# Pinning the order of sixteen seven-product units, with their input sums moved to VectorE and their SBUF pools laid out anew

## The chip, the core and the metric

The kernel runs on one core of one Trainium2 chip. The metric is the device time of one execution in microseconds. The core has TensorE (matrix products, written to eight banks of PSUM), VectorE (DVE in the profile), ScalarE (ACT), GpSimd (POOL) and queues that start transfers between memory and SBUF (SP's and GpSimd's here). Each engine takes its instructions in one fixed order, and waits at an instruction until what it needs is there.

## The reference, cut to what matters

Two layers over 1024 latent tokens and 256 context tokens, with 1024 features. The first layer is attention beside an mLSTM; the change lies at the start of the second, odd layer:

```python
def _c_mixer(h_lat, h_ctx, w_in, lb, h_norm, w_out, need_ctx):
    def project(h):
        q, f_fwd, f_bwd, i, z = _split_cols(h @ w_in, C_SIZES)   # five blocks of 2048 columns

        def decay(f_pre):
            f = lb + (1.0 - lb) * jax.nn.sigmoid(f_pre.astype(F32))
            return _bht(_heads(1.0 - f, HG_HEADS)), _bht(_heads(jnp.log(f), HG_HEADS))

        rec = (_bht(_heads(jax.nn.silu(q), HG_HEADS)), _bht(_heads(i, HG_HEADS)), (decay(f_fwd), decay(f_bwd)))
        return rec, z
    ...
```

`h` is the normed and modulated input of the layer. The part concerned computes two of the five blocks, `q` (with its SiLU, for the latent tokens) and `f_fwd` (with sigmoid and lower bound, for all tokens), for all 16 heads of 128 columns. The other blocks are computed later, head by head.

## The kernel before, in words

**Products in three parts.** Every float32 product is made of three matmuls on a split of each operand into a high and a low part: `split` (L68 on) writes the high part with a cast on ScalarE (L73) and the low part with a subtraction on VectorE (L74). `dense` issues, for each block of 128 features, high x high (L131), low x high and high x low (L132, L133). The input `h` lies split and transposed in SBUF as `hh` and `hl`, [128, 8, 1280]: eight blocks of 128 features, 1024 latent tokens and 256 context tokens.

**The stage in front.** The first layer ends with ten output tiles of 128 tokens, in the order 8, 9 (context), 4, 5, 6, 7, 0, 1, 2, 3. `out_tile` computes one: the products, then on VectorE `og` (L959, reads the bank) and the new `ox` (L960). `norm` makes `nx` (a square with sum on ScalarE, two small GpSimd instructions for the root, a scaling on VectorE, L282), and `mod_tr` transposes it on TensorE (L294) and writes `ntmp`, from which `h_sink` writes `hh` (ScalarE, L317) and `hl` (VectorE, L318). Tokens 0 to 511 come last; token tile 3 is the last of all. The weights of these products lie in the pool `wo1` (28 tiles), the other tiles of the stage in `op0`.

**The seven-product phase** (`hg_wide`). For `q` and `f_fwd` the latent tokens are cut in two halves of 512 (t = 0, 1), the 1024 features in two halves (c = 0, 1), and two heads' columns make a pair: a product of 2 x 2 blocks, done with seven block products in place of eight (Strassen's scheme in Winograd's form). One unit is one pair of heads of one kind; 16 units run in the order f, q, f, q, ... In each:

- P1 = X(0,0) by weight block (0,0) into bank `a`; the copy `p1` (L1151, ScalarE) keeps it; P2 = X(0,1) by block (1,0) is added into `a`, which then is output block (0,0).
- P4 = X(1,1) by the weight form t4 into a bank `d`.
- P6 = S2 by t2 into a bank `b`; VectorE makes `u2` = b + p1 (`add`, L1054); P7 = S3 by t3 is added into `b`; `u3` = b + p1. Output block (1,0) is d + u3.
- P5 = S1 by t1 into a bank `c`; output block (1,1) is c + u3; P3 = S4 by block (1,1) is added into `c`; output block (0,1) is c + u2.
- An f unit also computes its context tokens from the raw weight blocks, in four parts of 12 matmuls of 256 columns (`cpart`, bank `tr`), behind P1, P2, before P3 (C1 in the diff) and behind P3. A q unit has none.

A block product is 12 matmuls of 512 columns. Each result goes through a sigmoid on ScalarE, one instruction on VectorE and a transfer by GpSimd's queue to memory (`finish`), with tiles `co` from a ring of two.

S1 to S4 are sums of quarters of `h`, [128, 4, 512] each, split in `st1` to `st4` (h and l). `half_sums` computes them at the start: S1 = A(1,0) + A(1,1), S2 = S1 - A(0,0), S3 = A(0,0) - A(1,0), S4 = A(0,1) - S2, each A being hh + hl. S1, S2 and S4 run on VectorE (28 instructions, L1022 and L1024) in `gF`'s free half and two tiles; S3 runs on GpSimd (12 instructions). The weight forms t1 to t4 are differences of raw weight blocks, computed on GpSimd (`raws`, L1078) in a ring `br` of 11 tiles, and split into a ring of four slab pairs in the pool `w1`, three ahead of the product that uses them (`more`).

**Order.** Instructions are traced in program order; a scheduler with a model of the engines then decides the order of each engine's queue. It takes what its model says is ready, earlier traced work first; `urgent()` puts a block ahead of all other. `seg()` fixes an order: what it encloses on TensorE is issued after `last_pe`. Before, `last_pe` is None during `hg_wide`, so the order of the products is the scheduler's choice. `hg_f` traces three gate parts of head 0 (context, tokens 512 to 1023, tokens 0 to 511) ahead of the phase.

**Pools.** `st` (S1 to S4, 64 KB a partition) and `sx` (`br`, `u2`, `u3`, `co`, `p1`) are laid over the bytes of `op0` and `wo1`, in the order in which their tiles are first asked for; with `reuse_waits="tile"` a new tile waits only for the old tiles under it. The next pool, `hg`, lies over `st` and `sx` in turn. The banks of PSUM are two `mm`, two `tr` and four of the current phase (`x` here, then `s`); a phase's pool has no such option before.

Of the kernel before, what the change touches and what calls it, by code (L numbers as in the profile page):

```python
# [10 lines left out]
F32 = mybir.dt.float32  # L11
# [3 lines left out]
ALU = mybir.AluOpType  # L15
# [30 lines left out]
class Prog:  # L46
# [929 lines left out]
    def hg_f(self, h, pool, w=None):  # L976
# [8 lines left out]
        def part(t0, n):  # L985
# [3 lines left out]
            if self.pinned:  # L989
                self.last_pe = m  # L990
# [20 lines left out]
    def half_sums(self, pool, tp, F):  # L1011
        nc = self.nc
        hh, hl = self.hh, self.hl
        S = {n: [self.t(pool, [P, 4, 512], F32R, f"st{n}{c}", 1) for c in "hl"] for n in (4, 3, 1, 2)}
        x = [F[:, 0, 0:512], F[:, 0, 512:1024]] + [self.t(tp, [P, 512], F32, n, 1) for n in ("u2", "u3")]
# [31 lines left out]
        return S  # L1047


    def hg_wide(self, sp, tp, F):  # L1050
# [15 lines left out]
        def raws(kind, i):  # L1066
# [9 lines left out]
            def sub(x, y, out=None):  # L1076
                o = self.t(tp, [P, 512], F32, "br", self.brs) if out is None else out
                nc.gpsimd.tensor_tensor(out=o, in0=x, in1=y, op=ALU.subtract)  # L1078
# [9 lines left out]
        order = lambda kind: [(0, 0), (1, 0), "t4", "t2", "t3", "t1"] + ([(0, 1)] if kind == "f" else []) + [(1, 1)]  # L1088
        queue = [(u, n) for u in range(len(units)) for n in order(units[u][0])]
        rawd, forms = {}, {}  # L1090

        def more(n):
            for u, f in queue[:n]:
                if u not in rawd:
                    rawd[u] = raws(*units[u])
                hi, lo = [self.t(self.wp, [P, 512], F32R, "w" + c, self.slabs) for c in "hl"]
                self.split(hi, lo, rawd[u][f])
                forms[(u, f)] = _W([hi], [lo], 4, P)
            del queue[:n]

        more(3)
        S = self.half_sums(sp, tp, F)
        for u, (kind, i) in enumerate(units):
            def form(n):
                more(1)
                return forms.pop((u, n))

            def finish(t, c, x):
                h = 2 * i + c
                o = self.t(tp, [P, 512], F32, "co", 2)  # L1110
# [17 lines left out]
            def cpart(c, w, k0, stop):  # L1128
                if kind == "q":
                    return  # L1130
                if c not in ctx:
                    ctx[c] = self.ps("tr", [P, CTX])
                self.dense(
                    ctx[c], w.h, w.l, lambda k: hh[:, k0 + k, LAT:T], lambda k: hl[:, k0 + k, LAT:T], 4, not stop, stop
                )
                if stop:
                    h = 2 * i + c
                    o = self.t(tp, [P, 512], F32, "co", 2)[:, 0:CTX]
# [7 lines left out]
            p1, u2, u3 = [self.t(tp, [P, 512], F32, n, 2 if n == "p1" else 1) for n in ("p1", "u2", "u3")]  # L1146
            pa, pd = [self.ps("mm", [P, 512]) for _ in range(2)]
            pb, pc = [self.ps("x", [P, 512]) for _ in range(2)]
            w = form((0, 0))
            prod(pa, w, (0, 0), True)  # L1150
            nc.scalar.copy(p1, pa)  # L1151
            cpart(0, w, 0, False)
            w = form((1, 0))
            prod(pa, w, (0, 1), False)
            finish(0, 0, pa)
            cpart(0, w, 4, True)
            prod(pd, form("t4"), (1, 1), True)
            prod(pb, form("t2"), 2, True)
            add(u2, pb, p1)
            prod(pb, form("t3"), 3, False)  # L1160
            add(u3, pb, p1)
            tail(1, 0, pd, u3, p1)
            prod(pc, form("t1"), 1, True)
            tail(1, 1, pc, u3, u3)
            if kind == "f":
# [953 lines left out]
```

## Time and profile before

| | |
|---|---|
| Median of 3 runs | 3346.03 us (3344.75 to 3347.75) |
| Profiled execution, its own time | 3344.65 us |
| Span of that execution | 3342.7 us, 64833 instructions, mean clock 0.996 |
| Busy: TensorE (PE), its weight loads (PEld) | 3288.8 us (98%), 2921.1 us (87%) |
| Busy: VectorE, ScalarE, GpSimd | 2178.8 us (65%), 1457.4 us (44%), 833.3 us (25%) |
| Last output product ends, phase begins | about 1787 us |
| Phase ends, first strips of the next stage | about 2183 us, 2188 us |

In the lists of the profile, a group names the line of the code, the engine, the operation, the tile written and the tiles read ("out<-in"), then a count; times are microseconds from the start of the span, means of one instruction nanoseconds. A bracket at the end of a row of the timeline gives the idle time in front of the instruction and what ended it. The granted clock of TensorE is a share of its full clock. Matmuls overlap: one of 512 columns is listed with 0.39 us while the next starts 0.23 us after it. L1054 is `add`, L1151 the copy `p1`, L1071 the loads of raw weights.

### The profile page before, as it was taken

To read this page: it belongs to the slowest core of one execution; us is meant where nothing else is said; L and a number is where in the kernel's file an instruction comes from. 1 tells how busy PE (TensorE), PEld (TensorE's weight loads), DVE (VectorE), ACT (ScalarE), POOL (GpSimd) and SP (SyncE) were. 2 spreads that over 40 slices of the span, in tenths; PEclk is the share of its full clock that TensorE was granted. 3 is DMA by queue.
4 is the path that set the end of the run, shared out by engine and by line. 5 is a ranking of instruction groups with operands and counts; after the bars stand their busy time and mean duration, and the time that the engine had idled before them with its cause. 6 is when DMAs were issued, how large, how long until landed. Compare 5 with 4: busy or idle time off the path is not lost.

```text
span 3342.7 us, 64833 instructions
## 1 busy us (share of the span) xinstructions
PE 3288.8 (98%) x24814; PEld 2921.1 (87%) x24814; DVE 2178.8 (65%) x4965; ACT 1457.4 (44%) x3389; POOL 833.3 (25%) x1215
## 2 busy tenths in 40 slices
PE   7999999999999999999998999999999999999999
PEld 6699899988989888898886888889999999999977
DVE  5337666666655566787668654577677677677756
ACT  5335554455444444455454333333333433433443
POOL 2222222212211112221104433202322323233110
PEclk9999999999999999999999999999999999999999
DMA  7713222232233444444652333222322324334376
GB/s 247 243 51 85 85 70 81 68 94 82 75 89 102 149 125 123 132 134 144 214 170 77 106 104 104 92 80 77 110 85 93 113 81 111 94 85 107 92 210 163
DMA packets 338101, 379.80 MB, mean 114 GB/s; under 512 B 34600, under 2 KB 269800, under 8 KB 336768
## 3 DMA queue, kind: packets, MB, share of 16 engines
q1 hardware_dynamic: 286032, 236.73, 24.0%
q0 software_dynamic: 51760, 138.94, 13.3%
q8 instruction: 195, 3.19, 0.4%
q14 instruction: 114, 0.93, 0.1%
HBM read 272.31 MB, written 103.08 MB: 112 GB/s over the span
## 4 chain that ended last, share of the span: by engine, by line
PE 90%; DMA 3%; issue 2%; DVE 2%; ACT 1%; POOL 1%; SPq 1%; ACTq 0%; POOLq 0%; DVEq 0%
PE mm L131 16%; PE mm L132 16%; PE mm L133 16%; PE s L1295 4%; PE mm L923 3%; PE mm L924 3%; PE mm L925 3%; PE acc L861 2%; PE tr L841 2%; PE acc L633 2%; PE s L642 2%; PE x L133 2%; PE x L131 2%; PE x L132 2%; PE s L1366 1%
## 5 line engine op out<-in xcount | busy, mean ns | idle before, releaser
L131 PE MATMUL mm<-wh,hh 128*128 128x256 f32 (+1 forms) x1504 | 465.0, 309 | 2.1 <-DVE graw L1588 0.8
L132 PE MATMUL mm<-wl,hh 128*128 128x256 f32 (+1 forms) x1504 | 462.8, 308 | 0.0
L133 PE MATMUL mm<-wh,hl 128*128 128x256 f32 (+1 forms) x1504 | 460.2, 306 | 0.0
L131 PE MATMUL mm<-hh,wh 128*128 128x512 f32 (+1 forms) x1160 | 424.3, 366 | 4.7 <-DVE og L959 3.1
L133 PE MATMUL mm<-hh,wl 128*128 128x512 f32 (+1 forms) x1160 | 419.6, 362 | 0.6 <-DVE wl L74 0.6
L132 PE MATMUL mm<-hl,wh 128*128 128x512 f32 (+1 forms) x1160 | 419.4, 362 | 0.6 <-DVE hl L318 0.6
L131 PEld LDWEIGHTS mm<-wh,hh 128*128 128x128 f32 x1504 | 283.9, 189 | 21.5 <-ACT ev L352 3.4
L132 PEld LDWEIGHTS mm<-wl,hh 128*128 128x128 f32 x1504 | 283.9, 189 | 12.4 <-issue 0.7
L133 PEld LDWEIGHTS mm<-wh,hl 128*128 128x128 f32 x1504 | 283.7, 189 | 12.0 <-issue 0.5
L131 PE MATMUL mm<-wzh,hh 128*128 128x256 f32 x960 | 280.8, 293 | 0.0
L132 PE MATMUL mm<-wzl,hh 128*128 128x256 f32 x960 | 271.3, 283 | 0.0
L133 PE MATMUL mm<-wzh,hl 128*128 128x256 f32 x960 | 271.2, 282 | 0.0
L131 PEld LDWEIGHTS mm<-hh,wh 128*128 128x128 f32 x1160 | 218.7, 189 | 41.0 <-ACT ev L371 4.2
L133 PEld LDWEIGHTS mm<-hh,wl 128*128 128x128 f32 x1160 | 218.4, 188 | 34.4 <-DVE wl L74 1.3
L132 PEld LDWEIGHTS mm<-hl,wh 128*128 128x128 f32 x1160 | 218.9, 189 | 31.5 <-DVE hl L318 1.4
L131 PEld LDWEIGHTS mm<-wzh,hh 128*128 128x128 f32 x960 | 183.5, 191 | 2.0
L132 PEld LDWEIGHTS mm<-wzl,hh 128*128 128x128 f32 x960 | 184.1, 192 | 0.0
L133 PEld LDWEIGHTS mm<-wzh,hl 128*128 128x128 f32 x960 | 183.6, 191 | 0.0
L74 DVE TENSOR_TENSOR wl<-wraw,wh 128x512 fp32r<-128x512 f32 x176 | 120.2, 690 | 82.7 <-ACT wh L73 80.5
L1325 DVE TENSOR_TENSOR gQ<-gQ,gF 128x1024 f32<-128x1024 f32 x112 | 149.0, 1331 | 29.9 <-PE s L1295 29.9
L1330 ACT COPY gksel<-gK 128x1024 f32<-128x1024 f32 x96 | 110.3, 1149 | 119.4 <-DVE gK L1325 55.0
L73 ACT CAST wh<-wraw 128x512 fp32r<-128x512 f32 x176 | 107.7, 620 | 96.6 <-PE mm L132 24.6
(559 smaller groups left out, 8468.0 us busy)
## 6 DMA issues: line engine op xcount, KB each, us to landing
wraw<-in_wab_dram SPq DMA_DIRECT2D x108, 256.0 KB
wraw<-yd SPq DMA_DIRECT2D x92, 256.0 KB
br<-in_wc_dram SPq DMA_DIRECT2D x64, 256.0 KB
md<-ev POOLq DMA_DIRECT2D x60, 256.0 KB, 2.6
wraw<-in_wc_dram SPq DMA_DIRECT2D x120, 128.0 KB
mloz<-md SPq DMA_DIRECT2D x40, 256.0 KB
s<-gyt POOLq DMA_DIRECT2D x36, 256.0 KB, 5.2
adar<-in_wada_dram SPq DMA_DIRECT2D x16, 512.0 KB
```

Of the source, the lines that this page charges most:

```text
L73: m = nc.scalar.copy(hi, x)
L74: nc.vector.tensor_tensor(out=lo, in0=x, in1=hi.bitcast(F32), op=ALU.subtract)
L131: mm(ps, lhsT=lh(k), rhs=rh(k), start=(start and k == 0), stop=False, skip_group_check=skip)
L132: mm(ps, lhsT=lh(k), rhs=rl(k), start=False, stop=False, skip_group_check=skip)
L133: m = mm(ps, lhsT=ll(k), rhs=rh(k), start=False, stop=(stop and k == nk - 1), skip_group_check=skip)
L633: nc.tensor.matmul(num, lhsT=qc[:, j, :], rhs=C[d][:, j, :], start=False, stop=(j == 1))
L923: mm(ps, lhsT=yh[k], rhs=w.h(kk), start=(kk == 0), stop=False)
L924: mm(ps, lhsT=yh[k], rhs=w.l(kk), start=False, stop=False)
L925: mm(ps, lhsT=yl[k], rhs=w.h(kk), start=False, stop=(kk == 8 * len(qs) - 1))
L1295: return self.nc.tensor.matmul(out[s], lhsT=lhsT, rhs=rhs, start=True, stop=True, tile_position=(0, b * 64))
L1325: nc.vector.tensor_tensor(out=v, in0=v, in1=tot, op=ALU.mult)
L1330: m = nc.scalar.copy(ksel.rearrange("p (b s i) -> p b s i", s=2, i=h), pick(K))
```

## The change

It does six things.

1. S3's 12 instructions run on VectorE (`chain(nc.vector, ...)`), and so do the four differences of unit 0's raw weights; those of the other units stay on GpSimd.
2. `half_sums` becomes a generator in three stages: places for the sums, then S1's sums, then everything else, traced at three points.
3. The four forms for P4, P1, P2 of unit 0 and P1 of unit 1 are split first, as urgent work, into the bytes that `st4` takes afterwards. The other forms go through the ring of slabs as before, in the order of the new list `steps`; two are traced ahead, and one more at each product.
4. Every product, every context part and the gate parts of head 0 stand in `seg()`: TensorE's order is that of `steps`. Unit 0 begins with P4, both parts of C0 (its first context column), the gate part F for tokens 0 to 511, P1, P2; then come P1 and P2 of unit 1; then P6, P5, P7, C1, P3 of unit 0, the rest of unit 1, and from unit 2 on P1, P2, P4, P6, P7, P5, (C1), P3 unit by unit. In unit 0 the addition for output block (1,1) is made after P7.
5. `st2`, `st3`, a pad of 256 bytes, `co`, `p1` and `u2` lie in `st`; `st1`, `st4`, `br` and `u3` in `sx`. `co`, `p1`, `u2` and `u3` are asked for where they are first used.
6. The phase pools of PSUM get `reuse_waits="tile"`.

The diff, cut:

```diff
@@ hg_f, part()
-            if self.pinned:
-                self.last_pe = m
+            self.last_pe = m
@@ half_sums
-        S = {n: [self.t(pool, [P, 4, 512], F32R, f"st{n}{c}", 1) for c in "hl"] for n in (4, 3, 1, 2)}
-        x = [F[:, 0, 0:512], F[:, 0, 512:1024]] + [self.t(tp, [P, 512], F32, n, 1) for n in ("u2", "u3")]
+        two = lambda n: [self.t(pool if n in (2, 3) else tp, [P, 4, 512], F32R, f"st{n}{c}", 1) for c in "hl"]
+        S = {n: two(n) for n in (2, 3, 1)}
+        self.t(pool, [P, 64], F32, "pad", 1)
+        yield two(4)
+        S[4] = two(4)
+        x = [F[:, 0, 0:512], F[:, 0, 512:1024]] + [
+            self.t(tp, [P, 512], F32, "u3", 1), self.t(tp, [P, 512], F32, "br", self.brs)
+        ]
...
             chain(nc.vector, x[j], h, (l, add), (h2, add), (l2, add))
+        yield
+        for j in range(4):
             done(1, j, x[j])
...
-            y = self.t(tp, [P, 512], F32, "co", 2)
-            chain(nc.gpsimd, y, h, (l, add), (h2, sub), (l2, sub))
+            y = self.t(pool, [P, 512], F32, "co", 2)
+            chain(nc.vector, y, h, (l, add), (h2, sub), (l2, sub))
...
-        return S
+        yield S
@@ hg_wide
         def prod(ps, w, n, first):
             x = X(n)
-            self.dense(ps, w.h, w.l, x[0], x[1], 4, first, True, True)
+            with self.seg():
+                self.last_pe = self.dense(ps, w.h, w.l, x[0], x[1], 4, first, True, True)
...
-                nc.gpsimd.tensor_tensor(out=o, in0=x, in1=y, op=ALU.subtract)
+                eng.tensor_tensor(out=o, in0=x, in1=y, op=ALU.subtract)
...
+        order = lambda kind: ["P1", "P2", "P4", "P6", "P7", "P5"] + (["C1"] if kind == "f" else []) + ["P3"]
+        form_of = dict(P1=(0, 0), P2=(1, 0), P4="t4", P6="t2", P7="t3", P5="t1", C1=(0, 1), P3=(1, 1))
+        steps = [(0, n) for n in ("P4", "C0", "F", "P1", "P2")] + [(1, "P1"), (1, "P2")]
+        steps += [(0, n) for n in ("P6", "P5", "P7", "C1", "P3")] + [(1, n) for n in order("q")[2:]]
+        steps += [(u, n) for u in range(2, len(units)) for n in order(units[u][0])]
...
+        def split_form(u, n, hi, lo):
+            if u not in rawd:
+                rawd[u] = raws(*units[u], *([nc.vector] if u == 0 else []))
+            self.split(hi, lo, rawd[u][form_of[n]])
+            forms[(u, n)] = _W([hi], [lo], 4, P)
+
+        sums = self.half_sums(sp, tp, F)
+        spare = next(sums)
+        for i, (u, n) in enumerate(((0, "P4"), (0, "P1"), (0, "P2"), (1, "P1"))):
+            with self.urgent():
+                split_form(u, n, *[t[:, i, :] for t in spare])
+        queue = [x for x in steps if x[1] in form_of and x not in forms]
...
-        more(3)
-        S = self.half_sums(sp, tp, F)
-        for u, (kind, i) in enumerate(units):
+        more(2)
+        next(sums)
...
+            def P1():
+                t["a"] = self.ps("mm", [P, 512])
+                t["p1"] = self.t(sp, [P, 512], F32, "p1", 2)
+                w = form("P1")
+                prod(t["a"], w, (0, 0), True)
+                nc.scalar.copy(t["p1"], t["a"])
+                if u:
+                    cpart(0, w, 0, False)
+
+            def P2():
+                w = form("P2")
+                prod(t["a"], w, (0, 1), False)
+                finish(0, 0, t["a"])
+                if u:
+                    cpart(0, w, 4, True)
...
+            def P6():
+                t["b"] = self.ps("x", [P, 512])
+                t["u2"] = self.t(sp, [P, 512], F32, "u2", 1)
+                prod(t["b"], form("P6"), 2, True)
+                add(t["u2"], t["b"], t["p1"])
+
+            def P7():
+                t["u3"] = self.t(tp, [P, 512], F32, "u3", 1)
+                prod(t["b"], form("P7"), 3, False)
+                add(t["u3"], t["b"], t["p1"])
+                tail(1, 0, t["d"], t["u3"], t["p1"])
+                if u == 0:
+                    c22()
...
+        todo = {}
+        for u, n in steps:
+            if u not in todo:
+                todo[u] = unit(u, *units[u])
+            todo[u][n]()
+            if (u, n) == (0, "F"):
+                S = next(sums)
@@ build
-                self.last_pe, self.pinned = None, False
+                self.last_pe = None
                 FF = self.hg_f(0, None, wf)
-                for part in FF[2]:
+                for part in FF[2][:2]:
                     part()
...
-                    self.hg_wide(sp, tp, FF[0])
+                    self.hg_wide(sp, tp, FF[0], FF[2][2])
@@ _Banks.phase
-        with self.tc.tile_pool(name="ps" + "".join(tags), bufs=1, space=PSUM) as pool:
+        with self.tc.tile_pool(name="ps" + "".join(tags), bufs=1, space=PSUM, reuse_waits="tile") as pool:
```

P3, P4, P5 and C1 are written as functions in the same way, with the instructions that they had. `cpart`'s matmuls stand in `seg()` too, and its `co` tile comes from `sp`.

More of the change, by code (lines that the diff above doesn't have):

```diff
@@ new lines, in c22, with P5, C1, P3 @@
+            def c22():
+                tail(1, 1, t["c"], t["u3"], t["u3"])
+            def P5():
+                t["c"] = self.ps("x", [P, 512])
+                prod(t["c"], form("P5"), 1, True)
+                if u:
+                    c22()
+            def C1():
+                cpart(1, form("C1"), 0, False)
+            def P3():
+                w = form("P3")
+                prod(t["c"], w, 4, False)
+                tail(0, 1, t["c"], t["u2"], t["u2"])
+                cpart(1, w, 4, True)
```

60 lines of the change are left out of this document (19 added, 41 removed).

## The prediction

> **What bounds the kernel now.** I read the page first, then the busy time by windows around the seven-product phase, then what TensorE waited for there, then the engines' timelines.
>
> ```profile
> PE 90%; DMA 3%; issue 2%; DVE 2%; ACT 1%; POOL 1%; SPq 1%; ACTq 0%; POOLq 0%; DVEq 0%
> ```
>
> The chain that ended last is TensorE for 90%, so a microsecond of TensorE idleness inside the phase is a microsecond of the time. The windows show where the phase has any (window, length, then busy time of PE, PEld, DVE, ACT, POOL, then the granted clock):
>
> ```profile
> 1787.00:1863.00 76.00, 60.19 (x271) 47.99 (x270) 68.72 (x93) 32.02 (x66) 41.71 (x30) 0.91 0.20 62
> 1960.00:2160.00 200.00, 200.00 (x979) 168.37 (x978) 102.59 (x158) 69.79 (x121) 68.55 (x78) 1.00 0.31 101
> 2176.00:2194.00 18.00, 12.90 (x112) 10.80 (x111) 14.76 (x25) 6.18 (x10) 2.05 (x3) 0.82 0.55 176
> 1802.00:1805.00 3.00, 2.92 (x10) 2.40 (x11) 1.18 (x3) 1.61 (x5) 0.63 (x1) 0.50 0.00 0
> 1830.00:1840.00 10.00, 7.48 (x19) 5.80 (x20) 10.00 (x13) 3.06 (x7) 3.91 (x3) 0.53 0.20 59
> ```
>
> Three stages. The seam into the phase (1787 to 1863) has 15.8 us without a matmul and two stretches at half clock. The body (1960 to 2160) has none at all: 200.00 of 200.00 at clock 1.00. The seam out (2176 to 2194) has 5.1 us. So a better seam can win, and the body can only lose. The waits of TensorE in the first seam:
>
> ```profile
> PE x L132 <- DVE st2l L74: 6.5, 2, 5.3
> PE mm L131 <- DVE og L959: 3.1, 1, 3.1
> PE tr L294 <- DVE nx L282: 3.1, 1, 3.1
> PE x L133 <- DVE wl L74: 1.3, 1, 1.3
> PE mm L131 <- ACT p L1151: 1.0, 1, 1.0
> PE mm L132 <- DVE hl L318: 0.6, 2, 0.3
> PE mm L133 <- DVE wl L74: 0.3, 1, 0.3
> ```
>
> All but one end on VectorE. The half clock costs 2.92 x 0.50 + 7.48 x 0.47 = 5.0 us more. Seam in: 15.9 + 5.0 = 20.9 us that a perfect change could take away.
>
> **The change, part by part.** *Sums and raw differences to VectorE.* The first row is TensorE's first matmul after the last output product; the others show what VectorE does while GpSimd (POOL) works, and after it has stopped:
>
> ```profile
> 1787.10 0.28 PE L131 MATMUL mm<-hh,wh 128*128 128x256 f32 x1
> 1785.51 5.97 POOL L1078 TENSOR_TENSOR br<-br,br 128x512 f32<-128x512 f32 x4 [6.06 <-DMA br<-in_wc_dram]
> 1786.05 3.02 DVE L1022 TENSOR_TENSOR u<-hh,hl 128x512 f32<-128x512 f32 x2
> 1792.47 0.68 DVE L959 TENSOR_TENSOR og<-mm,gbc 128x512 f32<-128x512 f32 x1
> 1822.45 1.46 POOL L1022 TENSOR_TENSOR co<-hh,hl 128x512 f32<-128x512 f32 x1
> 1832.39 1.59 POOL L1024 TENSOR_TENSOR co<-co,hl 128x512 f32<-128x512 f32 x1
> 1832.79 1.75 DVE L74 TENSOR_TENSOR wl<-br,wh 128x512 fp32r<-128x512 f32 x1
> 1834.46 0.68 DVE L74 TENSOR_TENSOR st2l<-u,st2h 128x512 fp32r<-128x512 f32 x1
> ```
>
> The same VectorE subtraction takes 1.75 us beside a GpSimd sum and 0.68 us (a pitch of 0.60) without one. From 1821 to 1834 eight VectorE instructions ran so, 8 x 1.1 = 9 us; that is where the 6.5, the 1.3 and the half clock after them come from. Likewise the two u sums took 3.02 us, and og, the first step for the last token tile, began at 1792.47, with TensorE waiting 3.1 us for the bank that it empties. The change takes the 12 GpSimd sums away and adds 12 + 4 (raw differences of unit 0) VectorE instructions, 16 x 0.60 = 9.6 us: about what it saves in slow ones. GpSimd keeps the four differences of unit 1.
>
> *Pools.*
>
> ```profile
> 1760.92 0.69 DVE L1024 TENSOR_TENSOR gF<-gF,hl 128x512 f32<-128x512 f32 x1
> 1811.78 1.14 ACT L73 CAST st1h<-gF 128x512 fp32r<-128x512 f32 x2
> ```
>
> The sum S1 was finished in gF at 1761.6 and only split at 1811.78: its place lay over bytes still in use by the last token tile. In the new layout st1, st4 and the raw weights lie over old weight slabs, st2 and st3 (which need the last tokens anyway) over the token tiles. No work is added; S1, and four split forms kept in st4's bytes, move ahead of the last tokens. The raw loads of units 0 and 1 and the splits of the four forms become urgent: on SP's queue the loads pass only those of later weights, and on ScalarE and VectorE the splits stand before sums, not before og, which is ready later than they are.
>
> *The fixed order in the body.* This is the term that decides. Three banks are read in the middle of their accumulation: `a` by the copy p1 between P1 and P2, `b` by the addition of u2 between P6 and P7, `c` by the addition of block (1,1) between P5 and P3. Before, the scheduler was free to put another product there, and did (lines of TensorE, then VectorE):
>
> ```profile
> 1993.70 0.39 PE L133 MATMUL x<-st2h,wl 128*128 128x512 f32 x1
> 1993.93 0.39 PE L131 MATMUL x<-st1h,wh 128*128 128x512 f32 x1
> 1996.91 0.40 PE L131 MATMUL x<-st3h,wh 128*128 128x512 f32 x1
> 1994.13 0.69 DVE L1054 TENSOR_TENSOR u<-x,p 128x512 f32<-128x512 f32 x1 [1.65 <-PE x L133]
> ```
>
> P6 (st2) is followed by P5 (st1), and P7 (st3) starts 3 us later, when the addition is long done. The change chains each product behind the one before it, in the order P1, P2, P4, P6, P7, P5, [C1], P3: P7 directly behind P6, and in a q unit, which has no context parts, P2 directly behind P1 and P3 behind P5. TensorE's queue is in order, so all later products stand behind the waiting matmul. The price: the addition starts 1994.13 - 1993.70 = 0.43 us after the last matmul's start and takes 0.69. The rest from the two waits of this kind that the trace has:
>
> ```profile
> 2178.93 0.69 DVE L1054 TENSOR_TENSOR u<-x,u 128x512 f32<-128x512 f32 x1
> 2179.68 0.50 PE L131 MATMUL x<-st4h,wh 128*128 128x512 f32 x1 [0.56 <-DVE u L1054]
> 2180.02 0.39 PE L132 MATMUL x<-st4l,wh 128*128 128x512 f32 x1
> 1845.65 0.39 PE L133 MATMUL mm<-hh,wl 128*128 128x512 f32 x1
> 1847.06 0.50 PE L131 MATMUL mm<-hh,wh 128*128 128x512 f32 x1 [1.02 <-ACT p L1151]
> 1845.91 0.62 ACT L73 CAST wh<-br 128x512 fp32r<-128x512 f32 x1 [1.23 <-PE mm L132]
> 1846.43 0.58 ACT L1151 COPY p<-mm 128x512 f32<-128x512 f32 x1
> 2022.95 0.28 PE L133 MATMUL tr<-hh,wl 128*128 128x256 f32 x1
> 2023.07 0.28 PE L131 MATMUL tr<-hh,wh 128*128 128x256 f32 x1
> ```
>
> TensorE goes on 0.06 us after the addition's end (2179.62 to 2179.68), and its first matmul keeps the next one back 0.34 instead of 0.23. So a wait for VectorE costs 0.43 + 0.69 + 0.06 - 0.23 + 0.11 = 1.06 us. A wait for the copy: 1847.06 - 1845.65 - 0.23 + 0.11 = 1.29 us, with a cast of the next weights ahead of it on ScalarE (0.9 without). Count: P6-P7 in units 1 to 15, P5-P3 in the 8 q units: 23 for VectorE; P1-P2 in the 8 q units and in unit 0: 9 for ScalarE. In f units 12 x 0.12 = 1.4 us (the spacing of the last two rows) of context matmuls cover the other two. In unit 0 the addition for (1,1) comes third after P7: 0.43 + 2 x 0.60 + 0.69 + 0.06 - 0.23 - 1.4 = 0.8 us. Sum: 23 x 1.06 + 9 x 1.29 + 0.8 = **+36.8 us** where there was one wait of 1.0. Ends: 29 (0.95 and 0.82 each, no slow start, no cast ahead) and 48 (1.5 each: VectorE is half busy in the body, so an addition can find up to 0.6 us ahead of it).
>
> *Clock.* The 1.02-us wait left the clock alone; the 2.14-us wait in the seam out did not (the strips behind it took 1.98 us instead of 1.15):
>
> ```profile
> 1847.00:1850.00 3.00, 2.94 (x13) 2.44 (x14) 3.00 (x4) 0.12 (x2) 1.78 (x2) 1.00 0.14 49
> 2186.00:2189.00 3.00, 1.14 (x22) 1.17 (x24) 3.00 (x6) 1.54 (x2) 0.07 (x1) 0.74 0.90 233
> 2187.86 1.98 PE L1295 MATMUL s<-gq,gkn 128*64 128x64 f32 x32 [2.14 <-DVE gkn L1257]
> 2205.55 1.15 PE L1295 MATMUL s<-gQ,gksel 128*64 128x64 f32 x32 [0.32 <-DVE gQ L1325]
> ```
>
> So I take no clock loss for the new waits. The Trainium skill (TensorE: Matmul & The Clock Gate, "A second HAM failure mode: psum-queue depth-cycling") says otherwise: short idle times between groups of matmuls, made by cycling through PSUM, can swing the clock between half and full. By the row the sum below is +18.7 us, by that rule some 54 us more. The row at 1847 speaks against the rule for one such wait alone; what many in succession do no row shows, so it is a rival below.
>
> *Order in the seam.* After the last output product TensorE now has the gate of context and of tokens 512 up, P4 and the two context parts of unit 0, before anything with tokens 0 to 511. At 0.23 us and 0.12 us a matmul: 24 x 0.12 + 24 x 0.23 + 12 x 0.23 + 24 x 0.12 = 14 us. The three waits for og, nx and hl (6.8 us) should go. What is late next: S4, the last of the sums, behind everything on VectorE. From 1786 VectorE has about 64 instructions of pitch 0.60 (34 of sums, 16 low parts of sums, 10 of forms, 4 differences), 38 us, and some 20 mostly short ones for the last tokens and the gates, which I put at 8 us (an estimate, at 0.4 each): 1832. TensorE comes to P3 of unit 0 at 1787.1 + 14 + 1.0 (8 transposes) + 5.5 (gate of tokens 0 to 511) + 11 (four products) + 8.3 (P6, P5, P7) + 1.4 (C1) + 3.4 (waits for two copies and the 0.8 above) = 1831.7. That is a tie; four GpSimd differences beside it cost VectorE some 4 x 1.1 = 4.4 us, which I take as the wait left. Ends: 0 (they fall elsewhere) and 12 (twelve more slow instructions). **Seam in: -20.9 + 4.4 = -16.5.**
>
> *Seam out.* The first projection of the next stage, 2.9 us, now stands behind P3 of the last unit instead of filling gaps before it; the q load may start after P6 instead of after P3, but the tiles for the first level lie over the pool that the last unit still empties into memory. Of the 5.1 us idle I take 1.6 off, with ends of 6 off and 3 on. *PSUM pools by tile*: outside this phase the banks of a new pool were free long before; 0, and 2 either way.
>
> **Sum.** -16.5 + 36.8 - 1.6 = +18.7 us. The profiled execution took 3344.65 us (span 3342.7); that gives 3363.3. The runs' median lies 1.4 us higher than this execution, so 3364 for a median.
>
> **Rivals.** *The seams win* (faster): what decides is how many of the 32 waits in mid-accumulation stand bare. If other work lies between those products (if the chain of order does not hold the matmuls as I read it), nothing is paid and the seams' 18.1 us stay: 3326 to 3328. The break-even is 18.1 / 1.15, about 16 bare waits. For it: VectorE's waits are what the change attacks, and they are large. Against: the body has no other matmuls to put there. 0.12. *A draw*: waits at their lower end (29) and both seams closed entirely (-20.9 - 6): +2; with half of that good luck up to +8: 3342 to 3352. 0.10. *VectorE becomes the bound of the seam*: its tie with TensorE breaks and all 12 us come back, with waits at 1.5 each: -8.9 + 48 = +39: 3378 to 3385. 0.07. *The clock swings in the body*: if every wait brought what the 2.14-us one did (two groups of strips at 1.98 instead of 1.15 us before full speed was back, 1.7 us), 32 x 1.7 = 54 more: 3418. 0.03. The rest, 0.68, is my forecast, 3352 to 3378.
>
> **How the numbers follow.** The least that a measurement of this kernel can tell is about 0.2%, 6.7 us: 3339.3 to 3352.7. Faster: the first rival, 0.12. Same: the draw, 0.10, and 0.01 of my forecast's lower edge. Slower: the rest, 0.77. The range goes from the draw (3343) to the VectorE rival (3382), leaving out the faster case, the swinging clock and the tails.
>
> **What would show it.** Right: in the changed profile TensorE's waits list some 23 of about 0.8 us (the list counts from the modelled end of the last matmul, 0.16 us after the next could have started) under DVE's L1054 counterpart and 8 or 9 under the copy p1; a window of 200 us in the body shows TensorE some 16 us short of full; no GpSimd sums of hh and hl; VectorE's splits at 0.68 us in the seam; st1 written well before the last tokens; 1787 to the end of unit 1 shorter by over 10 us. Wrong: a body still at 200 of 200; waits of 1.7 us or a clock under 1.00 in the body; or a seam still waiting 10 us for st4 or st3.

## The result, and the profile after

The changed kernel takes 3375.66 us in the median of five runs (3375.44 to 3376.24), the kernel before 3345.07 us (3343.14 to 3347.75) on the same chip: ratio 1.0091, 95% interval 1.0076 to 1.0106, so 30.6 us slower. The profiled execution has a span of 3373.8 us where that of before had 3342.7. (Of the kernel e3 below, the profiled execution took 6571 us, nearly twice its other three; it is left out of that kernel's median, and no row of its profile is used.)

The page of the changed kernel, the chain that ended last:

```profile
PE 87%; DMA 4%; DVE 3%; issue 3%; ACT 1%; POOL 1%; SPq 1%; POOLq 0%; ACTq 0%; DVEq 0%
```

TensorE's share of the chain fell from 90% to 87%: it has the same matmuls as before, and most of the added time is waiting. Where it waits, the windows of the same kernel say (window, length, busy time of PE, PEld, DVE, ACT, POOL, then the granted clock):

```profile
1787.00:1863.00 76.00, 63.23 (x285) 49.94 (x284) 65.45 (x114) 34.25 (x72) 21.07 (x18) 0.91 0.29 89
1960.00:2160.00 200.00, 185.17 (x879) 150.51 (x878) 98.66 (x145) 65.06 (x111) 66.66 (x74) 1.00 0.27 91
2204.00:2222.00 18.00, 13.46 (x106) 11.29 (x105) 13.43 (x22) 6.53 (x10) 2.04 (x3) 0.88 0.45 136
```

The body, full before, lacks 14.8 us in 200. The seam in has 3.0 us more TensorE work in the same 76 us than before (63.23 against 60.19), and the same clock of 0.91. The third window is the seam out, which has moved from 2176 to 2204 or so. TensorE's waits in the changed kernel, over the whole span (name of the tile waited for, total, times, longest):

```profile
PE x L131 <- DVE u L1061: 19.5, 23, 0.9
...
PE mm L131 <- ACT p L1175: 8.7, 9, 1.0
PE x L131 <- ACT st3h L73: 4.2, 1, 4.2
...
PE s L1359 <- DVE gkn L1321: 2.7, 1, 2.7
PE s L1359 <- ACT gksel L1394: 1.9, 1, 1.9
PE tr L131 <- DVE ntmp L304: 1.7, 1, 1.7
PE tr L294 <- DVE nx L282: 1.6, 1, 1.6
PE x L133 <- DVE st4l L74: 1.1, 1, 1.1
PE x L131 <- ACT st4h L73: 1.1, 1, 1.1
```

L1061 is the addition `add` (L1054 before) and L1175 the copy `p1`. Twenty-three waits under the one and nine under the other: the list holds the two counts of the prediction to the unit. One of them in the timeline, TensorE's rows first and VectorE's addition last:

```profile
2201.31 0.40 PE L133 MATMUL x<-st2h,wl 128*128 128x512 f32 x1
2202.49 0.51 PE L131 MATMUL x<-st3h,wh 128*128 128x512 f32 x1 [0.78 <-DVE u L1061]
2202.84 0.40 PE L132 MATMUL x<-st3l,wh 128*128 128x512 f32 x1
...
2201.75 0.69 DVE L1061 TENSOR_TENSOR u<-x,p 128x512 f32<-128x512 f32 x1 [1.60 <-PE x L133]
```

P6 (st2) is followed at once by P7 (st3). The last matmul of P6 starts at 2201.31, the addition 0.44 us later, P7 0.05 us after the addition's end, and its second matmul 0.35 us behind its first: 2202.49 - 2201.31 - 0.23 + 0.12 = 1.07 us lost, where the prediction reckoned 1.06.

**The sum in the prediction's own terms.** Waits in mid-accumulation: 19.5 + 8.7 listed, and 32 x (0.16 + 0.11) around them, as worked out there: 36.8. Seam in: the waits between 1785 and 1870 that are not of this kind are the five rows from st3h down without gkn and gksel and 0.2 for st3l, 9.9 us, where before had 15.9; the half clock costs 4.9 us as before (rows below); so the seam gained 6.1. Seam out: 5.6 us of waits before, 5.6 after. 36.8 - 6.1 - 0 = 30.7, against 30.6 measured. The agreement is closer than the measurement can show: its interval is 25 to 35 us.

The seam is still long because VectorE's list of work ends late. VectorE in the changed kernel, then GpSimd (POOL), then TensorE:

```profile
1804.54 1.76 DVE L1027 TENSOR_TENSOR gF<-gF,hh 128x512 f32<-128x512 f32 x1
1806.22 2.36 DVE L74 TENSOR_TENSOR wl<-br,wh 128x512 fp32r<-128x512 f32 x2
...
1839.95 1.49 DVE L1136 TENSOR_SCALAR co<-co,lb 128x512 f32<-128x512 f32 x1
1841.36 1.75 DVE L1029 TENSOR_TENSOR co<-co,hl 128x512 f32<-128x512 f32 x1
1843.79 0.99 DVE L74 TENSOR_TENSOR st3l<-co,st3h 128x512 fp32r<-128x512 f32 x1 [0.68 <-ACT st3h L73]
...
1802.97 4.46 POOL L1086 TENSOR_TENSOR br<-br,br 128x512 f32<-128x512 f32 x3 [1.64 <-DVE st4l L74]
1837.12 7.11 POOL L1086 TENSOR_TENSOR br<-br,br 128x512 f32<-128x512 f32 x3 [18.90 <-DVE wl L74]
...
1843.81 0.79 PE L131 MATMUL x<-st3h,wh 128*128 128x512 f32 x1 [4.19 <-ACT st3h L73]
```

VectorE works nearly without a pause from 1787.5 to the end of S3's last quarter, 1844.8, 56.18 us of 57.30 and 98 instructions in all:

```profile
1787.50:1844.80 57.30, 45.59 (x205) 35.23 (x203) 56.18 (x98) 27.81 (x60) 17.07 (x12) 0.92 0.21 64
```

Beside GpSimd's raw differences for unit 1 (up to 1807.4) and unit 2 (from 1837.1) its instructions take 0.9 to 1.1 us more than the same forms elsewhere (the split of st3l, which overlaps them in part, 0.3 more), and two of them are the last steps of S3. TensorE stands in the middle of P7 for 4.2 us. The first waits of the seam (nx, then st4h and st4l) and the one for st3h have half clock behind them (windows of the changed kernel):

```profile
1801.00:1804.00 3.00, 1.71 (x4) 0.90 (x5) 3.00 (x6) 2.19 (x7) 1.36 (x2) 0.55 0.00 0
1804.00:1807.00 3.00, 3.00 (x9) 2.32 (x8) 3.00 (x3) 0.76 (x2) 3.00 (x3) 0.50 0.01 3
1844.00:1848.00 4.00, 3.77 (x14) 3.08 (x15) 3.32 (x5) 1.22 (x2) 1.80 (x4) 0.50 0.29 118
```

1.71 x 0.45 + 3.00 x 0.50 + 3.77 x 0.50 and 0.7 us at their edges: 4.9 us.

### The profile page after: what moved, and what is told of

It is laid out like the page before. It is cut to its first block, busy times and chain, and to the rows that moved or that the text cites. A ratio compares the mean times of both kernels' runs of the same rounds, so it can differ in the third digit from the quotient of the medians.

```text
span 3373.8 us, 64866 instructions
## 1 busy us (share of the span) xinstructions
PE 3295.2 (98%) x24814; PEld 2918.0 (86%) x24814; DVE 2178.4 (65%) x4981; ACT 1456.4 (43%) x3389; POOL 808.0 (24%) x1199
## 4 chain that ended last, share of the span: by engine, by line
PE 87%; DMA 4%; DVE 3%; issue 3%; ACT 1%; POOL 1%; SPq 1%; POOLq 0%; ACTq 0%; DVEq 0%
PE mm L131 16%; PE mm L132 15%; PE mm L133 15%; PE s L1359 4%; PE acc L861 2%; PE mm L923 2%; PE mm L924 2%; PE mm L925 2%; PE x L131 2%; PE tr L841 2%; PE x L133 2%; PE x L132 2%; PE acc L633 2%; PE s L642 2%; PE s L1430 1%
## 5 line engine op out<-in xcount | busy, mean ns | idle before, releaser
L131 PE MATMUL mm<-hh,wh 128*128 128x512 f32 (+1 forms) x1084 | 395.0, 364 | 8.0 <-ACT p L1175 8.0
L132 PE MATMUL mm<-hl,wh 128*128 128x512 f32 (+1 forms) x1084 | 389.6, 359 | 0.0
L133 PE MATMUL mm<-hh,wl 128*128 128x512 f32 (+1 forms) x1084 | 389.5, 359 | 0.0
L131 PEld LDWEIGHTS mm<-hh,wh 128*128 128x128 f32 x1084 | 204.3, 188 | 43.2 <-ACT p L1175 11.4
L133 PEld LDWEIGHTS mm<-hh,wl 128*128 128x128 f32 x1084 | 204.1, 188 | 29.9 <-issue 0.2
L132 PEld LDWEIGHTS mm<-hl,wh 128*128 128x128 f32 x1084 | 204.4, 189 | 26.7 <-issue 0.2
```

Source lines behind the costliest of these rows:

```text
L131: mm(ps, lhsT=lh(k), rhs=rh(k), start=(start and k == 0), stop=False, skip_group_check=skip)
L132: mm(ps, lhsT=lh(k), rhs=rl(k), start=False, stop=False, skip_group_check=skip)
L133: m = mm(ps, lhsT=ll(k), rhs=rh(k), start=False, stop=(stop and k == nk - 1), skip_group_check=skip)
```

## The experiments

Eleven kernels, in three groups; each group ran on one chip beside the kernel before. Medians, and the ratio to before with its 95% interval:

| kernel | us | ratio | interval |
|---|---|---|---|
| the change | 3375.66 | 1.0091 | 1.0076 to 1.0106 |
| e3_before_chained | 3377.3 | 1.0099 | 1.0083 to 1.0114 |
| e1_free_body | 3339.76 | 0.9989 | 0.9980 to 0.9998 |
| e2_covered | 3341.75 | 0.9991 | 0.9982 to 1.0000 |
| e4_p4_between | 3358.02 | 1.0038 | 1.0025 to 1.0051 |
| e8_before_sums_vector | 3340.46 | 0.9983 | 0.9974 to 0.9991 |
| e11_psum_by_tile | 3345.67 | 1.0000 | 0.9992 to 1.0009 |
| e5_p4_fill | 3343.61 | 0.9995 | 0.9986 to 1.0003 |
| e6_diffs_vector | 3339.64 | 0.9980 | 0.9972 to 0.9989 |
| e7_short_s3 | 3341.38 | 0.9986 | 0.9977 to 0.9995 |
| e9_seam_vector | 3336.74 | 0.9975 | 0.9966 to 0.9985 |
| e10_seam_order | 3330.55 | 0.9956 | 0.9942 to 0.9969 |

The kernel before had 3344.91, 3345.47 and 3345.21 us in the three groups. Single executions of one kernel lie up to 7 us from their median, so a difference of 2 us between neighbours in this table says little by itself. "The covered kernel" below is e2.

**The loss: is it the bare waits?** Theory: the fixed order makes 28 of the 32 waits in units 2 to 15, and they are the loss. Rival: something else that came with the change (pools, sums on VectorE).

*e3_before_chained* puts the order alone into the kernel before:

```
 def prod(ps, w, n, first):
     x = X(n)
-    self.dense(ps, w.h, w.l, x[0], x[1], 4, first, True, True)
+    with self.seg() if u > 1 else ExitStack():
+        m = self.dense(ps, w.h, w.l, x[0], x[1], 4, first, True, True)
+    if u > 1:
+        self.last_pe = m
...
```

The context parts are chained in the same way.

> The kernel before, with nothing but the chain of order added, for units 2 to 15, in its own written order (P1, P2, P4, P6, P7, P5, [C1], P3); seams, pools, sums as before. Theory (bare waits): 28 new waits, 32 us more than the kernel before: 3377 (3372 to 3382). Rival (pools, sums): no change, 3345, or under 3355.

It took 3377.3 us (three executions, 3376.94 to 3379.3), 32.4 more. The order alone does the whole harm.

*e1_free_body* takes it away from the changed kernel, for the same units:

```
-    with self.seg():
-        self.last_pe = self.dense(ps, w.h, w.l, x[0], x[1], 4, first, True, True)
+    with self.seg() if u < 2 else ExitStack():
+        m = self.dense(ps, w.h, w.l, x[0], x[1], 4, first, True, True)
+    if u < 2:
+        self.last_pe = m
...
```

The context parts likewise.

> The changed kernel with the chain of order kept for units 0 and 1 only; from unit 2 on the scheduler places the products itself, all else as changed. Theory (the loss is the 28 bare waits in mid-accumulation of units 2 to 15, 17.7 + 7.1 us listed and 28 x 0.27 = 7.6 us around them): 32 us less than the changed kernel, 3343 (3337 to 3348; products of unit 2 that may now fill the 4.2-us wait for st3 in the seam are the lower end). A 200-us window of the body has TensorE full again. Rival (the loss comes from the layout of pools, the PSUM pools by tile or the sums on VectorE): 3365 or more, with the waits still there under other names.

3339.76 us, 35.9 less than the change. The body is full again:

```profile
1960.00:2160.00 200.00, 200.00 (x975) 168.25 (x974) 101.12 (x158) 69.37 (x122) 66.21 (x77) 1.00 0.31 101
```

*e2_covered* keeps the chain and changes the order in it, so that no product follows directly the one into its own bank:

```
+covered = lambda kind: ["P1", "P6", "P2", "P5", "P7", "P4"] + (["C1"] if kind == "f" else []) + ["P3"]
-steps += [(u, n) for u in range(2, len(units)) for n in order(units[u][0])]
+steps += [(u, n) for u in range(2, len(units)) for n in covered(units[u][0])]
 def P4():
...
+    if u > 1:
+        tail(1, 0, t["d"], t["u3"], t["u3"])
 def P7():
...
+    if u > 1:
+        tail(1, 1, t["c"], t["u3"], t["p1"])
+    else:
+        tail(1, 0, t["d"], t["u3"], t["p1"])
...
```

> The changed kernel, still one chain of order, but from unit 2 on in the order P1, P6, P2, P5, P7, P4, [C1], P3, so that between every product and the next one into its bank stands another product (2.8 us); block (1,1) is added after P7 and block (1,0) after P4. Theory (bare waits): 28 waits go, 32 us less than the changed kernel: 3343 (3340 to 3348). Rival (a chain of order costs as such, by late forms or because the scheduler can no longer fill gaps): 3355 or more, with TensorE short of full in the body by other waits, for the forms wh and wl.

3341.75 us, 33.9 less than the change, and again a full body:

```profile
1960.00:2160.00 200.00, 200.00 (x981) 168.04 (x980) 108.10 (x157) 70.14 (x121) 67.28 (x78) 1.00 0.30 102
```

So a fixed order costs nothing as such. What costs is a product behind the one whose bank must be read first.

*e4_p4_between* swaps two names in the list, P4 and P6, from unit 2 on, which covers 14 of the 28:

```
-"P1", "P2", "P4", "P6", "P7", "P5"
+"P1", "P2", "P6", "P4", "P7", "P5"
```

> The changed kernel with one swap from unit 2 on: P6 before P4, so that P4 stands between P6 and P7. Theory (bare waits, 1.06 us of TensorE each for VectorE's addition): 14 of the 28 go, 14.8 us less than the changed kernel: 3361 (3358 to 3364), 9 waits left under the additions (19.5 - 14 x 0.85 = 7.6 us listed) and 9 under the copy p1. Rival (the price of a wait is not its own but that of falling behind, paid once per unit): less than 8 us, over 3368, the remaining waits grow longer.

3358.02 us, 17.6 less than the change, so 1.26 us for each wait, at the lower edge of what was expected. The list of its waits between 1785 and 2240:

```profile
PE mm L131 <- ACT p L1176: 8.7, 9, 1.0
PE x L131 <- DVE u L1061: 8.4, 10, 0.9
```

Ten waits under the addition where nine were reckoned, and the nine under the copy untouched. (The tenth, of 0.5 us, is in the seam.) The price belongs to the single wait: e1 gives 35.9 / 28 = 1.28, e2 1.21, e3 1.16, e4 1.26. The profile gives 32.4 / 28 = 1.16, the forecast 31.3 / 28 = 1.12. For e4, whose 14 waits are all for additions, the forecast was 1.06; its interval of 4 us either way leaves at least 0.3 either way on each wait, so these prices are not told apart.

**The gain that did not come.** Without its 28 waits the change should, by the forecast, have been 18.7 - 31.3 = 12.6 us faster than before. e1 and e2 are 5.2 and 3.2 us faster. The rest of the runs look for the missing 7 to 9 us in the seam.

*e8_before_sums_vector* moves only S3's sums in the kernel before:

```
-chain(nc.gpsimd, y, h, (l, add), (h2, sub), (l2, sub))
+chain(nc.vector, y, h, (l, add), (h2, sub), (l2, sub))
```

> The kernel before, with nothing but the 12 instructions of S3 moved from GpSimd to VectorE. The forecast's step (12 more instructions cost about what the slow ones beside GpSimd did, 7 us against 9): no change, 3345 (3342 to 3348), with VectorE's splits of st2 at 0.68 us and another wait in the place of st2l's 6.5. Rival A (the slow instructions were the cause of the 6.5-us wait and of the half clock behind it): up to 10 us less, 3335. Rival B (VectorE becomes the bound): 5 us more, 3350.

3340.46 us, 5.0 less than before. The 12 more instructions on VectorE do not cost what the contended instructions did; half of rival A came. The longest of its waits in the seam, 1785 to 1870:

```profile
PE mm L131 <- DVE og L959: 3.1, 1, 3.1
PE mm L131 <- ACT co L1111: 2.8, 1, 2.8
...
PE x L132 <- DVE st2l L74: 1.8, 1, 1.8
```

The 6.5 us for st2l are down to 1.8, and 2.8 us came back one step later, at the bank that the gate's sigmoid empties.

*e5_p4_fill*, on the covered kernel, gives TensorE other work while it waits:

```
-steps += [(0, n) for n in ("P6", "P5", "P7", "C1", "P3")] + [(1, n) for n in order("q")[2:]]
+steps += [(0, n) for n in ("P6", "P5")] + [(1, "P4")]
+steps += [(0, n) for n in ("P7", "C1", "P3")] + [(1, n) for n in order("q")[3:]]
```

> The covered order, and in the seam P4 of unit 1 (2.8 us, needs only token sums that are long there) moved ahead of P7 of unit 0, which waits 4.2 us for st3. Theory (in the seam VectorE's list of work is the bound up to the last quarter of S3; TensorE has idle time there that other work can fill): the wait shrinks to some 1.4 us and the time by 2.8 us against the covered order, 3339 (3336 to 3342). Rival (what is late next takes it back: st4 or the forms of unit 1): 3342, with the same idle time at other tiles.

3343.61 us, no gain: the rival. The two longest of its waits in the seam:

```profile
PE x L131 <- DVE u L1061: 3.6, 3, 1.8
PE x L131 <- ACT st3h L73: 2.3, 1, 2.3
```

The wait for st3 fell by 1.9 us and the one for the additions behind it rose by as much (1.7 in two waits before). Work put ahead of the wait helped nothing here, because the next thing hung on the same engine's list.

*e6_diffs_vector* lets GpSimd compute nothing beside the sums, on the covered kernel:

```
-rawd[u] = raws(*units[u], *([nc.vector] if u == 0 else []))
+rawd[u] = raws(*units[u], *([nc.vector] if u < 3 else []))
```

> The covered order, and the raw differences of units 1 and 2 on VectorE as those of unit 0, so that GpSimd computes nothing on large tiles in the seam. Theory A (GpSimd beside VectorE is what makes the seam long): slow VectorE instructions now cost 1.0 + 1.1 + 1.1 + 1.1 = 4.2 us at unit 1's differences and 2.3 at unit 2's; eight more instructions cost 4.8: S3's last quarter 1 to 2 us earlier, the time 1 to 2 us less than the covered order, 3340. Theory B (the mere number of VectorE instructions decides): 4.8 us more of them, S3's last quarter later, 3343 to 3346.

3339.64 us, 2.1 less than the covered kernel (3.7 by the two ratios). That is what theory A said, but the two intervals overlap, so the times alone do not decide. The trace does: S3's last quarter is split by 1840.4, where the covered kernel has 1843.0 (1841.97 + 0.99), though VectorE has eight more instructions. The last split, and TensorE's waits for S3 in the seam:

```profile
1839.70 0.69 DVE L74 TENSOR_TENSOR st3l<-co,st3h 128x512 fp32r<-128x512 f32 x1
...
PE x L132 <- DVE st3l L74: 2.7, 2, 2.5
PE x L131 <- ACT st3h L73: 1.7, 1, 1.7
```

The waits for S3 are no shorter, 4.4 us in all where the covered kernel has 4.6, because TensorE comes to them earlier too: the early wait for ntmp (1.7 us there) is gone, and the one for st4l fell from 1.5 to 0.4.

*e7_short_s3* takes instructions away instead. S3 is A(0,0) - A(1,0), and S2 is A(1,0) + A(1,1) - A(0,0), so S3 is also A(1,1) - S2:

```
-(h, l), (h2, l2) = A(0, 0, j), A(1, 0, j)
-chain(nc.vector, y, h, (l, add), (h2, sub), (l2, sub))
+h2, l2 = A(1, 1, j)
+chain(nc.vector, y, h2, (x[j], sub), (l2, add))
```

> The covered order, and S3 made from the finished S2 by two VectorE instructions a piece (block (1,1) less S2) in place of four: the same sum, rounded otherwise, with 8 fewer instructions of 0.60 us, 4.8 us. Theory B (the number of VectorE instructions decides): S3's last quarter is split at about 1838 in place of 1842, the 4.2-us wait for st3 falls to 0.5 or less, and the time is 4 us less than the covered order, 3338 (3335 to 3341). Rival (the ring of two places for S3's pieces and their place behind S4's in the queue hold st3 up): the wait stays over 2.5 us, the time within 1.5 us of the covered order.

3341.38 us, the rival's time, but by another way. S3's last quarter is split at 1836.2 to 1838.0 and no wait for st3 is left, as theory B had it. One wait has taken its place; TensorE, then VectorE, then GpSimd, in this kernel:

```profile
1845.28 0.51 PE L131 MATMUL x<-st4h,wh 128*128 128x512 f32 x1 [4.00 <-DVE u L1061]
...
1839.88 0.69 DVE L1061 TENSOR_TENSOR u<-x,p 128x512 f32<-128x512 f32 x1
1840.49 2.24 DVE L74 TENSOR_TENSOR wl<-br,wh 128x512 fp32r<-128x512 f32 x1
1842.65 0.68 DVE L1061 TENSOR_TENSOR p<-x,u 128x512 f32<-128x512 f32 x1
1843.25 1.37 DVE L74 TENSOR_TENSOR wl<-br,wh 128x512 fp32r<-128x512 f32 x1
1844.55 0.68 DVE L1061 TENSOR_TENSOR u<-x,u 128x512 f32<-128x512 f32 x1
...
1838.72 1.63 POOL L1086 TENSOR_TENSOR br<-br,br 128x512 f32<-128x512 f32 x1 [1.28 <-issue]
1840.88 1.29 POOL L1086 TENSOR_TENSOR br<-br,br 128x512 f32<-128x512 f32 x1
1842.81 1.27 POOL L1086 TENSOR_TENSOR br<-br,br 128x512 f32<-128x512 f32 x1 [0.64 <-DVE wl L74]
```

The addition of block (1,1), for which P3 waits, is the third of the three additions, behind two splits that GpSimd's differences slow to 2.24 and 1.37 us. (Additions that read one operand from PSUM keep their 0.68 us beside GpSimd.)

*e9_seam_vector* is e6 and e7 together.

> The covered order with both edits to the seam at once: differences of units 1 and 2 on VectorE, S3 from S2 in two instructions. VectorE has as many instructions as in the covered order (8 more, 8 fewer), and none beside GpSimd's. Theory (VectorE's list bounds the seam, by its instructions and by GpSimd's slowing of them together; each edit alone let the wait move on, to st3l, or to the addition of block (1,1) behind forms wl of 2.24 and 1.37 us): slow instructions of 4.2 + 2.3 us go, and with them the waits for st3 (4.2 us in the covered order) and the stretch at half clock behind it: 5 to 8 us less than the covered order, 3335 (3332 to 3338). Rival (the two edits do the same thing twice): as the better of the two alone, 3339 or more.

3336.74 us, 5.0 less than the covered kernel (5.4 by the ratios), at the lower end of what the theory said, and about the sum of what the two edits gave alone (3.7 and 1.7 by the ratios, neither clear of the noise). VectorE has as many instructions as there and none slow, S3's last quarter is split by 1834.7, and of the waits for st3 0.3 us is left. Still one wait is long, TensorE and then VectorE:

```profile
1841.96 0.80 PE L131 MATMUL x<-st4h,wh 128*128 128x512 f32 x1 [5.04 <-DVE u L1061]
...
1837.02 0.68 DVE L1061 TENSOR_TENSOR u<-x,p 128x512 f32<-128x512 f32 x1
1841.22 0.68 DVE L1061 TENSOR_TENSOR u<-x,u 128x512 f32<-128x512 f32 x1
```

The first of these additions is the one behind P7, the second the one that P3 needs. Between them lie six other instructions of VectorE, all at full speed, three of them raw differences that this kernel has on VectorE: a wait in mid-accumulation again, only a longer one.

*e10_seam_order* therefore gives units 0 and 1 the covered treatment as well:

```
+steps = [(0, n) for n in ("P4", "C0", "F", "P1")] + [(1, "P1"), (0, "P2"), (1, "P2")]
+steps += [(0, n) for n in ("P6", "P5", "P7")] + [(1, "P4")] + [(0, n) for n in ("C1", "P3")]
+steps += [(1, n) for n in ("P6", "P5", "P7")] + [(2, "P1"), (1, "P3")] + [(2, n) for n in covered("f")[1:]]
+steps += [(u, n) for u in range(3, len(units)) for n in covered(units[u][0])]
 def P7():
...
+    tail(1, 1, t["c"], t["u3"], t["p1"])
+    if u < 2:
+        tail(1, 0, t["d"], t["u3"], t["u3"])
...
```

> The kernel of the run before, and the covered idea carried into units 0 and 1: order of steps P1, P1 of unit 1, P2, P2 of unit 1, P6, P5, P7, P4 of unit 1, C1, P3, then P6, P5, P7 of unit 1, P1 of unit 2, P3; block (1,1) added before block (1,0). Theory (bare waits): two waits for the copy p1 (1.29 each) and the three for additions in these units (1.06 each, 0.8 for unit 0) go, 5 us less than the run before: 3330 (3327 to 3334). Rival (in the seam VectorE's list decides, and a covered wait only moves to the next one): within 2 us of the run before.

3330.55 us (3329.51 to 3332.62), 6.2 less than the run before it, 45.1 less than the change and 14.7 less than the kernel before. The waits in the seam for p1 (1.6 us in e9) and for the additions (6.8) are gone from its list, and one of 2.7 us for st3l stands there next. The seam's window of this kernel has 69.78 us of TensorE work in 76, where the change had 63.23:

```profile
1787.00:1863.00 76.00, 69.78 (x327) 56.60 (x326) 66.19 (x124) 36.54 (x75) 13.40 (x16) 0.96 0.29 90
```

*e11_psum_by_tile* tries the remaining part alone, in the kernel before:

```
-tile_pool(name="ps" + "".join(tags), bufs=1, space=PSUM)
+tile_pool(name="ps" + "".join(tags), bufs=1, space=PSUM, reuse_waits="tile")
```

> The kernel before, with nothing but the PSUM pools of a stage released by tile in place of all at once. The forecast's step: no change, 0 with 2 us either way, 3345. Rival (a share of the gain or the loss comes from it): beyond 2 us.

3345.67 us against 3345.21: no change that the interval (3 us either way) can show.

## Why the prediction was right, and which term was too large

**Fixed order in the body, +36.8: right, in kind, count and place.** 23 and 9 waits were forecast and 23 and 9 are listed; a 200-us window was to be 16 us short and is 14.8 short. e3 shows that the order alone does it, e2 that it does it only where a product stands bare, e4 that each wait has its own price. By the runs that price is 1.16 to 1.28 us, a little over the forecast's mean of 1.12; 28 times the difference is 1 to 4.5 us, inside the ends given. That the list of waits adds up to the same 36.8 is in part luck: the additions cost 1.12 each by the list where 1.06 was reckoned, the copies 1.24 where it was 1.29, and the 0.8 of unit 0 is not there.

**Clock: right.** The body kept 1.00 with its 28 waits. The rival that the Trainium skill suggested (TensorE: Matmul & The Clock Gate, "A second HAM failure mode: psum-queue depth-cycling") is refuted for idle times of 0.8 to 1.0 us that lie 5.8 us and more apart: 3418 us by that rule, 3375.66 measured.

**Seam in, -16.5: the step that was too large; about -6 was measured.** The prediction let VectorE finish its list at 1832 in a tie with TensorE and charged 4.4 us for GpSimd. The list ended at 1844.8. The large instructions on the list were counted almost rightly: 34 of sums, 16 low parts of sums and 4 differences as forecast, and 11 forms in place of 10. Of the 12.8 us between, GpSimd's slowing is about half, 6.5 us (the instructions of the five VectorE rows above, and L992 at 1.50 for 0.54 and L318 at 1.35 for 0.28), since unit 2's differences fall into the seam too. The list began at 1787.5 in place of 1786, 1.5 us (the last output product ends 1.8 us later in this execution). The instructions put at "some 20", 8 us, are 33, seven of them large, and take 10.3 us at their usual length, 2.3 more; the 65 large ones at 0.60 take 39 us in place of 38; and pauses are 1.1 us. Together 12.4. The forecast had 4.4 us for GpSimd, as the whole wait that would be left.

What is late next was named wrongly: S4, where it was the last quarter of S3, four operations long and in a ring of two places, with TensorE already at 1839.6. That VectorE's list, with GpSimd's slowing of it, sets the seam up to S3 is shown by the end of S3's last split: 1843.0 in the covered kernel, 1840.4 without GpSimd's differences (e6), 1838.0 with eight instructions fewer (e7), 1834.7 with both (e9). How much time each of the two is worth is not shown, since e6 and e7 lie within the noise of the covered kernel; both together gain 5.0 us.

That three early waits (nx 1.6, st4 2.2, ntmp 1.7) stayed, the first two with half clock behind them, was missed as well: the waits for nx and hl of before were to go entirely. Two likely causes stand in the trace. The raw weights from which P4's form is made now lie over the slabs of the output products: their load stood 14.3 us in SP's queue until the last matmul that reads those slabs (L925) and went out at 1786 in place of 1779, a price of the new layout that the prediction did not count. And the small GpSimd instruction ahead of nx (L157) took 1.78 us where it took 0.18 for the tile before, beside VectorE's run of splits and differences. Whether an earlier load would end these waits was not tried, nor GpSimd's root kept clear of that run.

The sign named beforehand, 1787 to the end of unit 1 shorter by over 10 us, did not come: unit 1's P3 ends at 1869.5 in place of 1877.7, and the kernel before had done two more products and two more context parts by then.

**Sums to VectorE, "about what it saves": too small a gain.** S3's sums alone are worth 5.0 us (e8), 3 to 9 by the interval, where 7.2 us of added instructions were set against about 9 lost beside GpSimd. The splits of st2 did take 0.68 us and the wait for st2l fell by 4.7; why the added instructions gave back only the 2.8 at the gate was not followed further.

**Seam out, -1.6: nothing came.** 5.6 us of waits before, 5.6 after. In the trace of before 18 matmuls of the next projection ran ahead of the wait at 2179.68, the first and the last of them:

```profile
2176.81 0.28 PE L131 MATMUL mm<-hh,wh 128*128 128x256 f32 x1
2178.84 0.28 PE L133 MATMUL mm<-hh,wl 128*128 128x256 f32 x1
```

In the changed kernel they come behind P3, whose first row, and the first strips of the next stage, are:

```profile
2209.16 0.47 PE L131 MATMUL x<-st4h,wh 128*128 128x512 f32 x1 [0.88 <-DVE u L1061]
...
2218.61 1.98 PE L1359 MATMUL s<-gq,gkn 128*64 128x64 f32 x32 [2.68 <-DVE gkn L1321]
```

9.45 us from the one to the other, 8.18 before (2179.68 to 2187.86), with 18 x 0.12 = 2.2 us of projection moved in between: 0.9 gained, and given back by the wait of 1.9 us for gksel. The chain keeps TensorE's fillers behind P3 while gkn comes no earlier after P3 than before.

**PSUM pools by tile, 0: right** (e11).

**The sum.** +18.7 was forecast and +30.6 came, with the sign and the deciding term right; 10.4 of the 11.9 us between lie in the seam in, 1.6 in the seam out. The rival in which VectorE becomes the bound of the seam was the right mechanism there, given only as an extreme.

## What to carry to other kernels

Before a scheduler's order is replaced by a fixed one, mark every bank that is read between two accumulations into it and place another product behind each such read: here the same seven products in another order (P1, P6, P2, P5, P7, P4, P3) from unit 2 on gave back 33.9 us, by the list of waits (32.4) all that the first order cost there, with the same tiles. A seam that hangs on one engine's list is shortened by taking work off that list or by ending what slows it (both together gave 5.0 us in e9), not by feeding the waiting engine something else; and an edit that ends one wait should be judged by the wait that stands there next, as e7 and e9 show. e10 does all of this and is the fastest of these kernels, 14.7 us under the one before.

## What the runs showed of the hardware that was not expected

GpSimd slows only some forms of VectorE's instructions, and those by about 1 us and more. In e7 a split with two operands in SBUF took 2.24 us and the addition from PSUM just ahead of it 0.69, both beside GpSimd subtractions of 1.3 to 1.6 us; in the changed kernel a multiplication by columns (L1136) took 1.49 in place of 0.54. The Trainium skill says the same (SBUF — State Buffer, "Who interferes with whom"): VectorE and GpSimd share one pair of ports, whoever has it keeps it for its whole instruction, a VectorE instruction with two inputs in SBUF contends and one with at most one does not, unless it runs in a mode that uses both ports. These rows agree on both kinds, the one that contends and the one that does not; that L1136 runs in such a mode no row here shows.

Twenty-eight idle times of 0.8 to 1.0 us, 5.8 us and more apart, left the clock at 1.00; two of 1.6 and 1.1 us (nx and st4h in the list of waits of the changed kernel), with 1.1 us of transposes between them, brought it to 0.55 and 0.50 for some 6 us. The one of 4.2 us brought it to 0.50, and so did a single one of 2.7 us in e10 (st3l; 0.50 from 1836 to 1838). Whether the length of one idle time or the idle share of a few microseconds decides, no run here tells.
